# Convolution sums in a PSUM bank, and products between the transposes of a feed-forward block: a two-layer hybrid encoder in float32

## The chip, the cores and the metric

The kernel runs on one core of a Trainium2 chip. The metric is the device time of one execution in microseconds (us); the median of three runs is compared. The engines are TensorE (PE, and PEld for its weight loads), VectorE (DVE), ScalarE (ACT), GpSimd (POOL) and SyncE (SP, which here only starts the weight loads).

## The reference, cut to what matters

Each of two layers works on x, 256 tokens by 1024 channels:

```python
x = x + 0.5 * swiglu_ffn(rms_norm(x, g1), w_gate, w_up, w_down)       # 1024 -> 2816 -> 1024
u = rms_norm(x, g_mix) @ w_in                                         # 1024 -> 2304
z = a * sigmoid(gate)                                                 # 256 channels each, from u
y_conv = silu(layer_norm(depthwise_conv(z, w_dw, width=31) + b_dw))
y_pool = pooled means (windows 2, 4, 8, 16) minus u, a linear map per group, a scale
y_attn = differential attention, 4 heads, softmax(q0 k0) - lam * softmax(q1 k1)
x = x + concat(y_conv, y_pool, y_attn) @ w_out
x = x + 0.5 * swiglu_ffn(rms_norm(x, g2), w_gate2, w_up2, w_down2)
x = rms_norm(x, g_post)
```

The change concerns two places of it: the depthwise convolution, 31 taps for each of 256 channels, and the turn of the hidden activation of the feed-forward block between its up and its down product.

## The kernel before, in words

All weights are streamed from HBM in pieces of 1 MB (`WeightStream`), and each quarter of a piece is split into a high and a low float32r part: ACT casts the high part (`whi`), DVE subtracts to get the low part (`wlo`). A product of float32 accuracy is then three matmuls, high by high, high by low, low by high (`mm3`), issued together.

A feed-forward block (`ffn`, tiles `f0a`, `f0b`, `f1a`, `f1b`: layer 0 or 1, first or second block) goes through the 2816 hidden channels in five chunks of 512 and one of 256. For each chunk it forms gate and up (`g`, `u`), multiplies them into `t`, and turns `t` on TensorE: per 256 channels four transposes of 128x128 fill one PSUM bank `hTr`, from which ACT and DVE take the high and low parts `hh` and `hl`. A chunk of 512 has eight such transposes, a block 44, the kernel 176. The down product `d` reads `hh` and `hl`.

The mixer (`mixer`, tiles `mx`) has the convolution, the pooling, the attention and the output product `w`. For the convolution a group of 128 channels (`conv(g)`, two of them) is projected (`mx_conv`), gated (`mx_ct`) and multiplied on GpSimd into a row padded by 15 on each side, `zpad`. Then 31 instructions on DVE, the taps, each multiply a shifted window of `zpad` by one column of the parameter tile `par` and add it to the running sum `cacc`, 128x256 float32 in SBUF. So each tap but the first (a TENSOR_SCALAR, which also adds the bias) is a SCALAR_TENSOR_TENSOR that reads `zpad` and `cacc` and writes `cacc`. The two groups give 62 taps in a layer. Meanwhile `pool()` computes the windowed means on GpSimd (`mx_s`, `mx_pd`). Attention is made of the projection `mx_qk`, its norm (`mx_qksq` on ACT, `mx_qkf`, `mx_qkn` on DVE), the transposes `mx_qkT`, their split `mx_qkh` and `mx_qkl`, the scores `mx_sc` and so on.

PSUM has eight banks of 128x512 float32: four with the tag `mm` for long products, and four with the tag `at` for everything else: `hTr`, `tr`, `qkT`, `sc`, `aT`, `o`, `cT`, `cB`, `po`.

The order of all instructions is made before anything is issued: `Program` records every operation with its reads and writes, and `schedule()` plans them with costs from `_cost`, four rounds of a backward pass and a greedy forward pass (`_forwards`). The forward pass takes, among the engines, the operation that can start first; among those of one engine that can start at the same time, the one of highest priority. It also knows how many slots each tag has, and lets an operation wait for a slot. The planned order of each engine is then fixed; each engine works in order and waits for semaphores. Since all operations are issued by one line, the profile shows L431 for nearly all of them, and tiles tell them apart.

Of the kernel before, what the change touches and what calls it, by code (L numbers as in the profile page):

```python
# [16 lines left out]
P = 128  # L17
# [178 lines left out]
class RecordedPool:  # L196
    def __init__(self, pool, bufs, psum=False):
        self.pool, self.bufs, self.psum = pool, bufs, psum

    def tile(self, shape, dt, tag, name, bufs=None):  # L200
        return RecordedTile(self.pool, shape, dt, tag, bufs or self.bufs, name, self.psum).view


ENGINES = ("tensor", "vector", "scalar", "gpsimd", "sync")
# [1 line left out]

class Op:
    __slots__ = ("engine", "cost", "calls", "preds", "succs", "tiles", "prio", "start", "end", "table", "left", "est",
                 "lag")


class Program:
# [5 lines left out]
    def __init__(self, tc, nc):  # L218
        self.tc, self.nc = tc, nc
        self.ops = []  # L220
        self.open = None
        self.chains = {}
        self.waits = []
        self.after = set()
        for e in ("tensor", "vector", "scalar", "gpsimd", "sync"):
            setattr(self, e, _Engine(self, e))

# [13 lines left out]
    def add(self, engine, call, cost, reads, writes, table, lag):  # L241
        i = len(self.ops)
        if self.open is None or self.open == "new":
            op = Op()
            op.engine, op.cost, op.calls, op.preds, op.succs, op.tiles = engine, 0.0, [], set(), [], []
            op.table, op.lag = table, lag
            self.ops.append(op)
            if self.open == "new":
                self.open = op
        else:  # L250
            op = self.open
            i -= 1
            assert op.engine == engine
        op.calls.append(call)
        op.cost += cost * (MARGIN if engine in ("vector", "scalar") else 1.0)
        op.preds |= self.after
        for v in self.waits:
            op.preds.update(j for j, _ in v.tile.writes)
        for v in reads:
            b = v.box()  # L260
            for j, w in v.tile.writes:
                if j != i and _overlap(b, w):
                    op.preds.add(j)
            v.tile.reads.append((i, b))
        for v in writes:
            b = v.box()
            for lst in (v.tile.writes, v.tile.reads):
                for j, w in lst:
                    if j != i and _overlap(b, w):
                        op.preds.add(j)  # L270
            v.tile.writes.append((i, b))
        for v in (*reads, *writes):
            if v.tile not in op.tiles:
                op.tiles.append(v.tile)
                v.tile.touches += 1
# [66 lines left out]
    def _forwards(self):  # L342
        ops, lat = self.ops, LAT
        order_in_tag, next_in_tag, slots = {}, {}, {}
        for op in ops:
            for t in op.tiles:
                if t not in order_in_tag:
                    key = (id(t.pool), t.tag)
                    n = next_in_tag.setdefault(key, 0)
                    order_in_tag[t] = (key, n)  # L350
                    next_in_tag[key] = n + 1
                    slots.setdefault(key, [0.0] * t.bufs)
        done_in_tag = dict.fromkeys(next_in_tag, 0)
        left = {t: t.touches for t in order_in_tag}
        allocated = set()
        pending = {e: [] for e in ENGINES}
        free = dict.fromkeys(ENGINES, 0.0)
        tables = None
        for i, op in enumerate(ops):
            op.left, op.est = len(op.preds), 0.0  # L360
            if not op.left:
                pending[op.engine].append(i)
        result = []
        loads = [i for i, op in enumerate(ops) if op.engine == "sync"]

        def slot_time(op):
            t_, want = 0.0, {}
            for t in op.tiles:
                if t in allocated:
                    continue  # L370
                key, n = order_in_tag[t]
                k = want.get(key, 0)
                if key[1] in IN_ORDER and n != done_in_tag[key] + k or len(slots[key]) <= k:
                    return None
                want[key] = k + 1
                t_ = max(t_, sorted(slots[key])[k] + lat)
            return t_

        while len(result) < len(ops):
            best = None  # L380
            for e, lst in pending.items():
                cand = []
                for i in lst:
                    if e == "sync" and i != loads[0]:
                        continue
                    s = slot_time(ops[i])
                    if s is not None:
                        cand.append((max(ops[i].est, s, free[e]), i))
                if not cand:
                    continue  # L390
                t0 = min(c[0] for c in cand)
                if best is None or t0 < best[0]:
                    i = max((c for c in cand if c[0] <= t0 + 1e-6), key=lambda c: (ops[c[1]].prio, -c[1]))[1]
                    best = (t0, e, i)
            assert best is not None, "no instruction can be issued"
            t0, e, i = best
            op = ops[i]
            pending[e].remove(i)
            if e == "sync":
                loads.pop(0)  # L400
            cost = op.cost
            if op.table is not None and op.table != tables:
                tables = op.table
                cost += 1.3
            op.start, op.end = t0, t0 + cost
            free[e] = op.end
            for t in op.tiles:
                if t not in allocated:
                    allocated.add(t)
                    key, _ = order_in_tag[t]  # L410
                    done_in_tag[key] += 1
                    slots[key].remove(min(slots[key]))
                left[t] -= 1
                if not left[t]:
                    slots[order_in_tag[t][0]].append(op.end + op.lag)
            for j in op.succs:
                o = ops[j]
                o.est = max(o.est, op.end + op.lag + (self.SAME[e] if o.engine == e else lat))
                o.left -= 1
                if not o.left:  # L420
                    pending[o.engine].append(j)
            result.append(i)
        return result
# [71 lines left out]
def trunk_kernel(  # L495
# [20 lines left out]
    def bank(name, tag="at"):  # L516
        return ps.tile([P, 512], F32, tag=tag, bufs=4, name=name)

    def slab_tile(name, dt=F32R):
        return slab.tile([P, 512], dt, tag="s", name=name)  # L520
# [41 lines left out]
    def pcol(l, c, n=1):  # L562
        return par[:, l * NPAR + c:l * NPAR + c + n]
# [95 lines left out]
    def ffn(norm, name, on_chunk, by_tokens=False):  # L659
# [11 lines left out]
        for j in range(NCH + 1):  # L671
# [21 lines left out]
                hid.append(s)  # L693
            for i in range(n // 256):
                tr = bank(f"{name}_hTr{j}{i}")
                for b in range(2):
                    for t in range(2):
                        nc.tensor.transpose(tr[:, b * 256 + t * P:b * 256 + (t + 1) * P],
                                            hid[t][:, (i * 2 + b) * P:(i * 2 + b + 1) * P], ident)
                hi, lo = slab_tile(f"{name}_hh{j}{i}"), slab_tile(f"{name}_hl{j}{i}")  # L700
                split(hi, lo, tr)
                hT += [(hi[:, :256], lo[:, :256]), (hi[:, 256:], lo[:, 256:])]
# [29 lines left out]
    def mixer(l, norm, neg_lam, q_gain, sub_gain, on_chunk):  # L732
# [16 lines left out]
            return acc  # L749

        cv = [tmp.tile([P, SEQ], F32, tag="cacc", name=f"{name}_cacc{g}") for g in range(2)]

        def conv(g):

            acc = proj_T(f"conv{g}")
            t = tmp.tile([P, 2, SEQ], F32, tag="gu", name=f"{name}_ct{g}", bufs=4)
            nc.vector.tensor_mul(t, acc.rearrange("p (a b) -> p a b", a=2),
                                 norm.r_bc.unsqueeze(1).to_broadcast([P, 2, SEQ]))
            nc.scalar.activation(t[:, 1], t[:, 1], AF.Sigmoid)
            nc.gpsimd.tensor_tensor(zpad[g][:, PADC:PADC + SEQ], t[:, 0], t[:, 1], op=ALU.mult)  # L760
            for i in range(CW):
                w = pcol(l, C_DW + g * CW + i)
                src = zpad[g][:, i:i + SEQ]
                if i == 0:
                    nc.vector.tensor_scalar(cv[g], src, w, pcol(l, C_DWB + g), op0=ALU.mult, op1=ALU.add)
                else:
                    nc.vector.scalar_tensor_tensor(
                        out=cv[g], in0=src, scalar=w, in1=cv[g], op0=ALU.mult, op1=ALU.add)

        def conv_norm():  # L770

# [391 lines left out]
```

## Time and profile before

| | us |
|---|---|
| median of 3 runs | 963.55 (962.37 to 964.35) |
| the profiled execution: time | 963.92 |
| its span, first to last instruction | 962.1 |
| PE busy, of the span | 938.0 |
| DVE busy | 611.9 |
| ACT busy | 522.9 |
| POOL busy | 62.5 |

The span is what the trace shows; the profiled execution's own time is 1.8 us longer, and 0.4 us above the median of the runs. A step saved in the span is taken to be saved in the time. The mean granted clock of TensorE over the span is 0.992 of full speed.

### The profile page before, as it was taken

How to read it: one execution, taken by the hardware profiler on the slowest of the kernel's cores; microseconds unless marked ns; L12 is line 12 of the kernel's file. 1: busy time of each engine (PE TensorE's matmuls, PEld its weight loads, DVE VectorE, ACT ScalarE, POOL GpSimd, SP SyncE). 2: the span in 40 equal slices, each digit the busy share in tenths (PEclk: the TensorE clock that was granted, in tenths of full speed). 3: DMA queues.
4: the chain of work that ended last, by engine and by line, in shares of the span. 5: the costliest groups of instructions: out<-in, count | busy, mean ns of one | idle time of the engine just before them, and what ended most of it. 6: DMA issues, size and time to landing. Idle time of an engine off the chain costs nothing.

```text
span 962.1 us, 13147 instructions
## 1 busy us (share of the span) xinstructions
PE 938.0 (97%) x4496; PEld 777.8 (81%) x4496; DVE 611.9 (64%) x1152; ACT 522.9 (54%) x1139; POOL 62.5 (6%) x81
## 2 busy tenths in 40 slices
PE   7999999998999999999999999999989999999997
PEld 5888888896778888888888888888967788888885
DVE  6765566659997555576645556665799865555612
ACT  7754445543886644555544455555369764554601
POOL 1000000014210000000000000000412100000000
PEclk9999999999999999999999999999989999999999
DMA  8885658640167555567516556775303655556601
GB/s 293 293 281 190 198 179 276 212 141 19 66 188 265 161 186 195 186 199 267 194 66 197 179 193 192 243 234 169 109 0 133 218 175 197 193 179 200 216 1 44
DMA packets 47907, 171.42 MB, mean 178 GB/s; under 512 B 5344, under 2 KB 5600, under 8 KB 47712
## 3 DMA queue, kind: packets, MB, share of 16 engines
q1 hardware_dynamic: 46656, 167.27, 52.4%
q0 software_dynamic: 608, 2.62, 0.8%
q8 instruction: 35, 0.57, 0.2%
q10 hardware_dynamic: 576, 0.70, 0.2%
q14 instruction: 32, 0.26, 0.1%
HBM read 169.52 MB, written 1.05 MB: 177 GB/s over the span
## 4 chain that ended last, share of the span: by engine, by line
PE 89%; DVE 5%; ACT 3%; issue 1%; DMA 1%; POOL 0%; SPq 0%; POOLq 0%
PE f0a_d L431 6%; PE f0b_d L431 6%; PE f1a_d L431 6%; PE f0a_g L431 6%; PE f0b_g L431 6%; PE f1b_g L431 6%; PE f1a_g L431 6%; PE f1b_u L431 6%; PE f0b_u L431 6%; PE f1a_u L431 6%; PE f0a_u L431 6%; PE f1b_d L431 5%; DVE mx_cacc L431 4%; PE mx_w L431 3%; PE mx_conv L431 2%; PE mx_v L431 2%
## 5 line engine op out<-in xcount | busy, mean ns | idle before, releaser
L431 DVE SCALAR_TENSOR_TENSOR mx_cacc<-zpad,par,mx_cacc 128x256 f32<-128x256 f32 x120 | 56.9, 542 | 0.1
L431 DVE TENSOR_TENSOR f0b_t<-f0b_t,f0b_u 128x512 f32<-128x512 f32 x10 | 6.8, 685 | 25.6 <-PE f0b_u L431 18.7
L431 DVE TENSOR_TENSOR f1b_t<-f1b_t,f1b_u 128x512 f32<-128x512 f32 x10 | 6.8, 685 | 25.0 <-PE f1b_u L431 18.7
L431 ACT ACT_TABLE_LOAD x12 | 15.4, 1283 | 13.2 <-PE f0b_g L431 5.8
L431 DVE SCALAR_TENSOR_TENSOR x<-f1b_d,f1b_rh,x 128x512 f32<-128x512 f32 x4 | 3.0, 750 | 29.3 <-PE f1b_d L431 29.3
L431 POOL DMA_DIRECT2D mx_pwr<-in_pool_w x2 | 1.2, 618 | 310.8 <-PE f1a_d L431 172.3
L431 ACT ACTIVATE fin_sq<-x 128x512 f32<-128x512 f32 x4 | 2.5, 632 | 34.3 <-DVE x L431 34.3
L431 ACT CAST f1a_hh<-f1a_hTr 128x512 fp32r<-128x512 f32 x11 | 6.0, 590 | 26.0 <-PE f1a_hTr L431 26.0
L431 ACT ACTIVATE f1a_t<-f1a_g,n1a_r 128x512 f32<-128x512 f32 x10 | 6.8, 690 | 23.4 <-PE f1a_g L431 23.4
L431 DVE TENSOR_TENSOR f1a_t<-f1a_t,f1a_u 128x512 f32<-128x512 f32 x10 | 6.8, 684 | 18.7 <-PE f1a_u L431 18.7
L431 ACT CAST f1b_hh<-f1b_hTr 128x512 fp32r<-128x512 f32 x11 | 6.0, 590 | 23.2 <-PE f1b_hTr L431 23.2
L431 ACT CAST f0b_hh<-f0b_hTr 128x512 fp32r<-128x512 f32 x11 | 6.0, 590 | 22.9 <-PE f0b_hTr L431 22.9
L431 DVE TENSOR_TENSOR f0a_t<-f0a_t,f0a_u 128x512 f32<-128x512 f32 x10 | 6.8, 684 | 16.9 <-PE f0a_u L431 16.9
L431 POOL TENSOR_TENSOR mx_qkf<-mx_qkf,mhalf 128x8 f32<-128x8 f32 x8 | 14.1, 1777 | 41.5 <-DVE mx_qkf L431 41.5
L431 ACT ACTIVATE mx_e<-mx_e,mx_mx 128x256 f32<-128x256 f32 x32 | 16.1, 506 | 0.6 <-DVE mx_mx L431 0.5
L431 ACT ACTIVATE f1b_t<-f1b_g,n1b_r 128x512 f32<-128x512 f32 x10 | 6.7, 689 | 16.4 <-PE f1b_g L431 16.4
L431 ACT ACTIVATE f0b_t<-f0b_g,n0b_r 128x512 f32<-128x512 f32 x10 | 6.7, 689 | 16.4 <-PE f0b_g L431 16.4
L431 ACT ACTIVATE mx_qksq<-mx_qk 128x64 f32<-128x64 f32 x64 | 13.2, 258 | 4.0 <-PE mx_qk L431 3.9
L431 PE MATMUL mx_qkT<-cst,mx_qkn 128*128 128x128 f32 x32 | 6.8, 303 | 7.5 <-DVE mx_qkn L431 7.5
L431 ACT CAST f0a_hh<-f0a_hTr 128x512 fp32r<-128x512 f32 x11 | 6.0, 590 | 14.9 <-PE f0a_hTr L431 14.8
L431 DVE CUSTOM_DVE_ANT_0 mx_e<-mx_sc,cst 128x256 f32<-128x256 f32 x32 | 12.3, 418 | 2.5 <-PE mx_sc L431 2.5
L431 POOL TENSOR_TENSOR fin_r<-fin_r,mhalf 128x1 f32<-128x1 f32 x2 | 1.9, 934 | 181.3 <-DVE fin_r L431 181.3
(4339 smaller groups left out, 3476.7 us busy)
## 6 DMA issues: line engine op xcount, KB each, us to landing
x<-in_x SPq DMA_DIRECT2D x4, 256.0 KB, 4.9
cst<-in_consts POOLq DMA_DIRECT2D x1, 1024.0 KB, 10.7
post<-in_post_rows POOLq DMA_DIRECT2D x2, 512.0 KB, 3.9
raw0a<-in_weights SPq DMA_DIRECT2D x2, 256.0 KB, 5.3
raw0b<-in_weights SPq DMA_DIRECT2D x2, 256.0 KB, 6.3
raw1a<-in_weights SPq DMA_DIRECT2D x1, 512.0 KB, 7.2
raw1b<-in_weights SPq DMA_DIRECT2D x1, 512.0 KB, 7.9
raw2a<-in_weights SPq DMA_DIRECT2D x1, 512.0 KB, 8.3
```

Source lines behind the costliest of these rows:

```text
L431: getattr(getattr(self.nc, engine), method)(*[a.resolve() if isinstance(a, View) else a for a in args], **{k: a.resolve() if isinstance(a, ...
```

## The change

The running sums of both groups of the convolution now lie in one PSUM bank, `csum`, with the tag `at`, one half for each group; the planner treats the halves as separate. The taps read the sum from PSUM and write it there, except that the last tap of a group writes its result to `cacc` in SBUF as before. `zpad` and `par` stay in SBUF, and the number and the order of taps stay. The bank is taken with the first tap and comes free with the last.

The transposes into `hTr` are marked `apart`. Where the planner has just put a transpose on TensorE, it takes an `apart` transpose next only if nothing else can start at that time. And it now counts 0.04 us more for a transpose that follows a transpose (`_cost` has 0.07 us for each).

```diff
-    def tile(self, shape, dt, tag, name, bufs=None):
-        return RecordedTile(self.pool, shape, dt, tag, bufs or self.bufs, name, self.psum).view
+    def tile(self, shape, dt, tag, name, bufs=None, whole=None):
+        return RecordedTile(self.pool, shape, dt, tag, bufs or self.bufs, name, self.psum if whole is None else whole).view
...
+    @property
+    def transpose(self):
+        return self.calls[0][1] == "transpose"
...
+        transposed = False
...
-                    i = max((c for c in cand if c[0] <= t0 + 1e-6), key=lambda c: (ops[c[1]].prio, -c[1]))[1]
+                    ready = [c for c in cand if c[0] <= t0 + 1e-6]
+                    if e == "tensor" and transposed:
+                        ready = [c for c in ready if not ops[c[1]].apart] or ready
+                    i = max(ready, key=lambda c: (ops[c[1]].prio, -c[1]))[1]
...
             cost = op.cost
+            if e == "tensor":
+                cost += 0.04 if transposed and op.transpose else 0.0
+                transposed = op.transpose
...
                 tr = bank(f"{name}_hTr{j}{i}")
+                nc.apart = True
                 for b in range(2):
                     for t in range(2):
                         nc.tensor.transpose(tr[:, b * 256 + t * P:b * 256 + (t + 1) * P],
                                             hid[t][:, (i * 2 + b) * P:(i * 2 + b + 1) * P], ident)
+                nc.apart = False
...
         cv = [tmp.tile([P, SEQ], F32, tag="cacc", name=f"{name}_cacc{g}") for g in range(2)]
+        cv_sum = ps.tile([P, 512], F32, tag="at", bufs=4, name=f"{name}_csum", whole=False)
...
                 src = zpad[g][:, i:i + SEQ]
+                acc = cv_sum[:, g * SEQ:(g + 1) * SEQ]
                 if i == 0:
-                    nc.vector.tensor_scalar(cv[g], src, w, pcol(l, C_DWB + g), op0=ALU.mult, op1=ALU.add)
+                    nc.vector.tensor_scalar(acc, src, w, pcol(l, C_DWB + g), op0=ALU.mult, op1=ALU.add)
                 else:
                     nc.vector.scalar_tensor_tensor(
-                        out=cv[g], in0=src, scalar=w, in1=cv[g], op0=ALU.mult, op1=ALU.add)
+                        out=acc if i < CW - 1 else cv[g], in0=src, scalar=w, in1=acc, op0=ALU.mult, op1=ALU.add)
```

## Rows read from the trace of the kernel before

**Rows 1.** The page: busy time of each engine; the chain, by engine.

```profile
PE 938.0 (97%) x4496; PEld 777.8 (81%) x4496; DVE 611.9 (64%) x1152; ACT 522.9 (54%) x1139; POOL 62.5 (6%) x81
...
PE 89%; DVE 5%; ACT 3%; issue 1%; DMA 1%; POOL 0%; SPq 0%; POOLq 0%
```

**Rows 2.** By stretch: us; busy PE, PEld, DVE, ACT, POOL; clock; DMA; GB/s.

```profile
9.00:201.50 192.50, 192.50 (x894) 160.37 (x894) 123.55 (x205) 111.85 (x208) 5.21 (x8) 1.00 0.71 235
201.50:290.00 88.50, 83.23 (x479) 69.10 (x478) 80.23 (x202) 58.33 (x189) 22.40 (x27) 0.98 0.31 103
...
673.00:768.00 95.00, 89.94 (x500) 74.23 (x499) 83.63 (x207) 60.51 (x193) 23.07 (x23) 0.95 0.34 114
```

**Rows 3.** Waits of PE, whole span: us in total, times, longest.

```profile
PE mx_qkT L431 <- DVE mx_qkn L431: 7.5, 2, 3.8
```

**Rows 4.** The chain that ended last: start us, us, what.

```profile
67.49 10.88 PE f0a_u L431 x48
...
216.26 17.48 DVE mx_cacc L431 x33
```

**Rows 5.** By stretch, instructions on `mx_cacc` alone: us; PE, PEld, DVE, ACT; clock.

```profile
215.80:225.34 9.54, 0.00 (x0) 0.00 (x0) 9.49 (x13) 0.00 (x0) 1.00 0.18 69
225.34:233.66 8.32, 0.00 (x0) 0.00 (x0) 8.32 (x22) 0.00 (x0) 1.00 0.00 2
```

**Rows 6.** Busy time of all engines in the first of these stretches.

```profile
215.80:225.35 9.55, 9.55 (x44) 7.90 (x43) 9.52 (x15) 0.41 (x1) 8.64 (x12) 1.00 0.18 69
```

**Rows 7.** Timeline of DVE and of POOL from 213 us: start us, us, instruction.

```profile
212.58 0.68 DVE L431 TENSOR_TENSOR wlo40d<-raw40b,whi40d 128x512 fp32r<-128x512 f32 x1
213.18 0.69 DVE L431 TENSOR_TENSOR mx_ct<-mx_conv,n0m_rbc 128x512 f32<-128x512 f32 x1
213.78 0.79 DVE L431 TENSOR_TENSOR wlo41d<-raw41b,whi41d 128x512 fp32r<-128x512 f32 x1
...
213.27 0.74 POOL L431 TENSOR_TENSOR zpad<-mx_ct 128x256 f32<-128x256 f32 x1 [12.19 <-ACT mx_ct L431]
```

**Rows 8.** Groups by form: xcount | busy us, mean ns | idle before us.

```profile
L431 DVE TENSOR_TENSOR f0a_hl<-f0a_hTr,f0a_hh 128x512 fp32r<-128x512 f32 x11 | 7.2, 685 | 2.3 <-ACT f0a_hh L431 2.3
L431 DVE SCALAR_TENSOR_TENSOR mx_e<-mx_e,mx_w 128x256 f32<-128x256 f32 x16 | 7.1, 477 | 0.0
...
L431 DVE SCALAR_TENSOR_TENSOR mx_qkl<-mx_qkT,par,mx_qkh 128x256 fp32r<-128x256 f32 x8 | 3.8, 474 | 0.4 <-ACT mx_qkh L431 0.4
...
L431 DVE TENSOR_TENSOR mx_ya<-mx_osb,mx_ya 128x256 fp32r<-128x256 f32 x8 | 3.3, 418 | 0.2 <-ACT mx_ya L431 0.2
```

**Rows 9.** Last square sum on ACT, then first norm step on DVE (timeline).

```profile
228.57 0.32 ACT L431 ACTIVATION_READ_ACCUMULATOR mx_qksq<-mx_qk 128x1 f32 x1
...
233.66 0.16 DVE L431 TENSOR_TENSOR mx_qkf<-mx_qkms,mx_em 128x8 f32<-128x8 f32 x1
```

**Rows 10.** By stretch, just after the wait, first and second mixer; columns as in 2.

```profile
237.30:240.40 3.10, 3.08 (x9) 2.53 (x10) 3.10 (x8) 0.00 (x0) 0.08 (x1) 0.52 0.00 0
...
708.90:714.50 5.60, 5.60 (x16) 4.44 (x17) 5.21 (x13) 0.84 (x2) 0.82 (x1) 0.50 0.00 0
```

**Rows 11.** Timeline of DVE: first scores, first and second mixer, with idle before.

```profile
247.97 0.42 DVE L431 CUSTOM_DVE_ANT_0 mx_e<-mx_sc,cst 128x256 f32<-128x256 f32 x1 [0.62 <-PE mx_sc L431]
...
720.83 0.42 DVE L431 CUSTOM_DVE_ANT_0 mx_e<-mx_sc,cst 128x256 f32<-128x256 f32 x1 [0.94 <-PE mx_sc L431]
```

**Rows 12.** Timeline of PE: runs of `hTr` transposes, three products after each.

```profile
134.48 1.03 PE L431 MATMUL f0a_hTr<-cst,f0a_t 128*128 128x128 f32 x8
...
136.06 0.27 PE L431 MATMUL f0a_hTr<-cst,f0a_t 128*128 128x128 f32 x1
...
136.87 0.38 PE L431 MATMUL f0a_hTr<-cst,f0a_t 128*128 128x128 f32 x2
...
137.78 0.27 PE L431 MATMUL f0a_hTr<-cst,f0a_t 128*128 128x128 f32 x1
```

More of the change, by code (lines that the diff above doesn't have):

```diff
@@ L208 @@
     __slots__ = ("engine", "cost", "calls", "preds", "succs", "tiles", "prio", "start", "end", "table", "left", "est",
-                 "lag")
+                 "lag", "apart")
+    @property
+    def transpose(self):
+        return self.calls[0][1] == "transpose"
 class Program:
@@ L224, in __init__ @@
         self.after = set()
+        self.apart = False
         for e in ("tensor", "vector", "scalar", "gpsimd", "sync"):
@@ L245, in add @@
             op.engine, op.cost, op.calls, op.preds, op.succs, op.tiles = engine, 0.0, [], set(), [], []
-            op.table, op.lag = table, lag
+            op.table, op.lag, op.apart = table, lag, self.apart
             self.ops.append(op)
```

## The prediction

> **What bounds the kernel now.** I read the page first. PE is busy 97% of the span and holds 89% of the chain that ended last [rows 1], so two questions matter: does the change shorten PE's own work, and does it remove idle time of PE. The table by stretch answers where such idle time is. In the first feed-forward block PE is busy 192.50 of 192.50 us [rows 2], and so it is in the others; there only the length of PE's instructions counts. In the mixers PE is busy 83.23 of 88.50 and 89.94 of 95.00 us, 5.3 and 5.1 us idle, while DVE is busy 80.23 and 83.63 us [rows 2]. The list of waits then names the place: 7.5 us in two waits of up to 3.8, one in each mixer, the transposes `mx_qkT` waiting for DVE's `mx_qkn` [rows 3]. And the chain says what DVE was doing: 17.48 us of it in one piece are taps [rows 4]. So in the mixer the taps stand ahead of what PE waits for.
>
> Then I looked at the taps by themselves. In the 9.54 us from 215.80 there are 13, one every 0.73 us; in the 8.32 us after it 22 are counted, of which the first is the end of the thirteenth, so 21 at 0.396 us [rows 5]. The instructions are the same. What differs is GpSimd: in the slow stretch it is busy 8.64 of 9.55 us with its 12 instructions of the gate and the pooling [rows 6], in the other not at all. The second mixer repeats this, 13 taps in the 9.54 us from 687.35. So 13 taps in each mixer are held up by GpSimd, by 9.54 - 13 x 0.396 = 4.4 us.
>
> Is it every DVE instruction that GpSimd holds up? The two instructions beside the multiply into `zpad`, which reads and writes SBUF, say no: `mx_ct`, which has one input in PSUM, began at 213.18 and took 0.69 us although GpSimd worked from 213.27; the next, a subtract with both inputs in SBUF, took 0.79, where the same subtract at 212.58, before GpSimd began, took 0.68 [rows 7]. One pair is thin evidence, but it points to the second input from SBUF.
>
> **The change, part by part.** *Taps beside GpSimd.* With the sum in PSUM a tap has one tensor in SBUF, `zpad`, and the column of `par`. If the hold-up goes, each mixer's DVE gains the 4.4 us. If it stays, because `zpad` or the column is enough to cause it, the gain is 0: these are the two bounds. I take 4.4, since `mx_ct` also had one SBUF tensor and was not held up.
>
> *Taps in general.* 62 taps in a mixer now read and write PSUM. For reading there are rows: a SCALAR_TENSOR_TENSOR of 256 elements takes 474 ns with one input in PSUM (`mx_qkl`) and 477 with both in SBUF (`mx_e`) [rows 8]. Nothing on DVE writes PSUM in this trace. Lower bound: 3 ns less, that is 0.2 us a mixer. Upper bound: the bank cannot be read and written at once, and the stream of 256 elements passes twice; 256 elements are worth 685 - 418 = 267 ns on a two-input instruction [rows 8], so 62 x 0.267 = 16.6 us a mixer. I take 0, the value for reading, which is the row it is nearest to. The 0.396 us of an undisturbed tap come from a chain in which each tap reads what the one before wrote, so a wait for the write in SBUF is in them already.
>
> [...] The rows on reading do not show a loss (474 against 477 ns), and no row here shows a write. [...]
>
> *What DVE's 4.4 us are worth.* What DVE does next in the first mixer is `mx_qkf` at 233.66. Its input from ACT was done at 228.9 [rows 9]; 4.4 us earlier is 229.3, so DVE does not run into ACT. `mx_qkn` follows 4.4 us earlier too, and PE's wait of 3.8 us goes. With it goes a second loss. In undisturbed work 48 products of 512 columns take 10.88 us, 0.227 each [rows 4]. [...] So PE could be ahead by 3.8 + 1.5 = 5.3 us in the first and 6.6 us in the second mixer, more than DVE's 4.4. DVE is therefore what is late next, and sets the gain: 4.4, plus the waits of DVE for the first scores, 0.62 and 0.94 us [rows 11], which vanish, as PE is 0.9 and 2.2 us further ahead than DVE. That gives 5.0 and 5.3 us. I carry all of it to the end of the mixer, because DVE is the busiest engine after PE there (80.23 of 88.50 us [rows 2]) and each step behind it moves with it; weight loads move too, as they wait for buffers that DVE empties.
>
> *The bank.* Four banks `at` become three while the taps run, from 215.8 to 247.3. In that time only the transposes `mx_qkT` of two heads need banks; the first scores come right after the last tap (248 [rows 11]). I cost it at 0, covered by that order. If the scores had to wait for the bank they would lose what they gain over the taps, at most 5.3 - 4.4 = 0.9 us a mixer.
>
> *Transposes.* The trace has both arrangements. From the start of a run of transposes to the next, with three products between: 134.48 to 136.06 with eight transposes, 136.06 to 136.87 with one, 136.87 to 137.78 with two [rows 12]. Three products are 3 x 0.227 = 0.68. So eight transposes cost 0.90 us, 0.112 each; two 0.23; one alone 0.13. A run costs 0.11 us for each transpose and 0.01 to 0.02 for being a run. The chain shows the 176 transposes in 47 runs (5 of eight, 15 of six, 19 of two, 8 single). If all stood alone there would be 129 more runs: 129 x 0.01 = 1.3 us more, up to 2.6. A single transpose is not cheaper, as the planner's 0.07 against 0.11 would have it. The bound below is that price, 129 x 0.04 = 5.2 us less; I take 1.3 more, from the rows. The later `hh` and `hl` cost nothing: they are read a whole chunk of products later, by the down product.
>
> The sum: 5.0 + 5.3 - 1.3 = 9.0 us off the profiled 963.92, so 954.9; its median is 0.4 lower. I say **954.6 us**.
>
> **The rivals.**
> *A dearer write to PSUM (slower).* Speaks for it: no row shows the write. Against: reading is no dearer. The gain of 10.3 us is gone when 124 taps each cost 0.08 us more (0.396 to 0.48); from there the change is a loss. At the upper bound it is 33 - 10 + 1.3 = 24 us slower, 988; at half of it 971.
> *The hold-up stays (no change).* GpSimd would hold up an instruction with one tensor and a column from SBUF. Speaks for it: `mx_ct` has no column. Then only the transposes count: 963.55 + 1.3 = 964.9.
> *Given back later.* DVE's gain shrinks in a new plan (the bank at its 0.9 us a mixer, another order of norm and taps, with PE's wait only partly gone). At a third to two thirds of 10.3 us: 958 to 962.
> *Single transposes are cheaper* between gate and up products, of which no single one stands in the trace: 963.6 - 10.3 - 5.2 = 948.
>
> **How the numbers follow.** Forecast 0.60; given back 0.13; hold-up stays 0.10; dearer write 0.12; cheaper transposes 0.05. What this kernel's measurement can tell from no change is about 0.2%, 1.9 us: faster means below 961.6. Faster: 0.60 + 0.13 + 0.05 = 0.78; within it: 0.10; slower: 0.12. The forecast's own range is 951 to 958 (bank lost, 1.8; transposes 1.3 dearer; on the other side all of PE's 11.9 us won and no loss on transposes). The range goes on through "given back" to the case without a change and leaves out the dearer write and most of the cheaper transposes: 949.5 to 965.
>
> **What the profile after would show.** Right: the 13 taps beside GpSimd at 0.40 us, as the others; no wait `mx_qkT <- mx_qkn` of microseconds; clock 1.00 after it; products 0.227 apart. `hTr` mostly single, each 0.12 to 0.13 us with its neighbours; feed-forward blocks 0.3 us longer. Wrong: taps at 0.45 us or more away from GpSimd (dearer write); taps still at 0.7 beside it (hold-up stays); a new wait for a bank or on ACT in 230 to 250 us; feed-forward blocks shorter by over 1 us (cheaper transposes).

## The result, and the profile after

The change made the kernel slower. Its median is 968.95 us (968.64 to 969.21, 4 runs) against 963.95 (962.37 to 964.52, 4 runs) for the kernel before, measured on the same chip: a ratio of 1.0054, with a 95% interval of 1.0037 to 1.0072. The prediction was 954.6 us and a range of 949.5 to 965.0, and the time lies above both. The profiled execution has a span of 966.8 us, 4.7 more than before.

First the page of the kernel after: busy time of each engine, then the chain by engine, to be laid beside [rows 1].

```profile
PE 941.3 (97%) x4496; PEld 772.8 (80%) x4496; DVE 614.0 (64%) x1152; ACT 523.1 (54%) x1139; POOL 58.2 (6%) x81
...
PE 86%; DVE 6%; ACT 3%; issue 2%; DMA 1%; POOL 0%; SPq 0%; POOLq 0%; DVEq 0%
```

PE's share of the chain fell from 89% to 86%, DVE's rose from 5% to 6%, and "issue" from 1% to 2%. So the wait for DVE has grown. The list of waits of PE says so directly (total, times, longest):

```profile
PE mx_qkT L443 <- DVE mx_qkn L443: 11.3, 2, 5.6
...
PE mx_aT L443 <- DVE mx_al L443: 0.5, 2, 0.3
PE mx_o L443 <- POOL mx_of L443: 0.3, 2, 0.2
PE mx_o L443 <- ACT mx_osb L443: 0.3, 1, 0.3
```

The wait that was to vanish went from 7.5 us [rows 3] to 11.3, one of about 5.6 in each mixer. What stands ahead of it are still the taps. They are on record in the list of the tile's instructions (durations in ns: least, median, most), and in the timeline of DVE (start us, us, instruction, count):

```profile
L443 DVE SCALAR_TENSOR_TENSOR mx_csum<-zpad,par,mx_csum x116: 478/490/491, 217.3 to 724.9; 128x256 f32<-128x256 f32 x116
```

```profile
216.73 0.54 DVE L443 TENSOR_SCALAR mx_csum<-zpad,par 128x256 f32<-128x256 f32 x1
217.30 0.49 DVE L443 SCALAR_TENSOR_TENSOR mx_csum<-zpad,par,mx_csum 128x256 f32<-128x256 f32 x1
217.90 0.55 DVE L443 TENSOR_SCALAR mx_csum<-zpad,par 128x256 f32<-128x256 f32 x1
218.48 16.77 DVE L443 SCALAR_TENSOR_TENSOR mx_csum<-zpad,par,mx_csum 128x256 f32<-128x256 f32 x32
235.16 0.16 DVE L443 TENSOR_TENSOR mx_qkf<-mx_qkms,mx_em 128x8 f32<-128x8 f32 x1
235.29 1.01 DVE L443 SCALAR_TENSOR_TENSOR mx_csum<-zpad,par,mx_csum 128x256 f32<-128x256 f32 x2
```

From the row of 32 taps one reads the distance of their starts: the last record is 0.49 long, so (16.77 - 0.49) / 31 = 0.525 us. Before, it was 0.73 on the mean beside GpSimd and 0.396 elsewhere [rows 5]. Now it is 0.525 everywhere, beside GpSimd too. That is two results in one. The hold-up is gone: no tap of the 116 is longer than 491 ns, though GpSimd is busy for 5.95 of the first 6.82 us of that row, as the table by stretch shows (columns as in [rows 6]):

```profile
218.48:225.30 6.82, 6.82 (x32) 5.65 (x31) 6.37 (x13) 0.41 (x1) 5.95 (x10) 1.00 0.04 14
```

And each tap now stands by itself. Before, records were 0.475 long and began 0.396 apart, so that they overlapped, as two taps of the second mixer show, which together take 0.87:

```profile
696.90 0.87 DVE L431 SCALAR_TENSOR_TENSOR mx_cacc<-zpad,par,mx_cacc 128x256 f32<-128x256 f32 x2
```

Now a record of 0.490 ends 0.035 us before the next begins. The chain, from 220.06, shows the same as pieces of DVE with "issue" between them (start us, us, what):

```profile
220.06 0.50 DVE mx_csum L443
220.56 0.02 issue
220.59 0.50 DVE mx_csum L443
221.09 0.02 issue
221.11 0.50 DVE mx_csum L443
```

The arithmetic for a mixer: 13 taps gain 0.73 - 0.525, in all 2.7 us; the other 49 lose 0.525 - 0.396 = 0.129 each, in all 6.3. DVE is 3.6 us later instead of 4.4 earlier. Measured, the stretch of the taps, from the first start to the last, grew by 3.2 us in the first mixer (215.82 to 246.88 before, 216.73 to 251.03 after).

PE does not wait for all 62 taps, but for `mx_qkn`. Ahead of its first instruction stand 41 taps before and 43 after, because the planner's order has changed too. So 13 taps gain 2.7, 28 lose 3.6, and two more take 1.05: 2.0 us later, by this sum. From the first tap to `mx_qkn` the traces have 20.77 us before and 22.63 after, 1.9 more, in either mixer, which is what each of PE's two waits has grown by. In before and in after:

```profile
236.59 0.68 DVE L431 TENSOR_TENSOR mx_qkn<-mx_qk,mx_qkf 128x512 f32<-128x512 f32 x1
239.36 0.68 DVE L443 TENSOR_TENSOR mx_qkn<-mx_qk,mx_qkf 128x512 f32<-128x512 f32 x1
```

Last the clock, by stretch, just behind the wait in either mixer (columns as in [rows 2]):

```profile
239.50:245.50 6.00, 5.40 (x15) 4.33 (x16) 5.47 (x12) 0.62 (x2) 0.00 (x0) 0.51 0.01 3
714.50:719.50 5.00, 4.59 (x13) 3.62 (x14) 4.75 (x11) 0.00 (x0) 0.00 (x0) 0.50 0.00 0
```

Behind PE's 5.6 us of idle time the granted clock is again about half, 0.51 over 6.00 us and 0.50 over 5.00, and in the first mixer for longer than before [rows 10].

Where the 4.7 us of span lie, by the starts of the same PE instructions in both traces (the last `mx_conv` product of a layer, the first `f0b_g` or `f1b_g` product behind the mixer):

| stretch | before | after | |
|---|---|---|---|
| to the last `mx_conv`, layer 0 | 212.73 | 213.64 | +0.91 |
| first mixer, to `f0b_g` | 82.43 | 84.67 | +2.24 |
| `f0b`, `f1a`, to the last `mx_conv`, layer 1 | 389.12 | 390.15 | +1.03 |
| second mixer, to `f1b_g` | 85.10 | 85.18 | +0.08 |
| to the end | 192.76 | 193.20 | +0.44 |

In the second mixer the longer wait is offset, because before has there a further stretch at the lower clock, which after does not have. In before:

```profile
759.50:762.50 3.00, 3.00 (x9) 2.33 (x8) 2.75 (x6) 2.24 (x5) 0.00 (x0) 0.50 0.87 289
```

and in after, in the same part of the mixer:

```profile
763.60:766.70 3.10, 3.10 (x16) 2.52 (x15) 3.10 (x7) 1.93 (x4) 0.69 (x1) 1.00 0.97 308
```

The row of before is worth 0.50 x 3.0 = 1.5 us; PE had been busy 3.21 of the 4.50 us ahead of it (755.0 to 759.5). The first row of the table is no effect of the change alone: four of the kernels below, whose instructions up to there are those of before, differ by 0.28 to 0.88.

### The profile page after: what moved, and what is told of

Read it like the earlier page. It is cut to its first block, busy times and chain, and to the rows that moved or that the text cites. A ratio compares the mean times of both kernels' runs of the same rounds, so it can differ in the third digit from the quotient of the medians.

```text
span 966.8 us, 13104 instructions
## 1 busy us (share of the span) xinstructions
PE 941.3 (97%) x4496; PEld 772.8 (80%) x4496; DVE 614.0 (64%) x1152; ACT 523.1 (54%) x1139; POOL 58.2 (6%) x81
## 3 DMA queue, kind: packets, MB, share of 16 engines
HBM read 169.52 MB, written 1.05 MB: 176 GB/s over the span
## 4 chain that ended last, share of the span: by engine, by line
PE 86%; DVE 6%; ACT 3%; issue 2%; DMA 1%; POOL 0%; SPq 0%; POOLq 0%; DVEq 0%
PE f1a_d L443 6%; PE f0a_d L443 6%; PE f0b_d L443 6%; PE f0a_g L443 6%; PE f1b_g L443 6%; PE f0b_g L443 6%; PE f1a_g L443 6%; PE f1b_u L443 6%; PE f0b_u L443 6%; PE f1a_u L443 6%; PE f0a_u L443 6%; PE f1b_d L443 5%; DVE mx_csum L443 5%; PE mx_w L443 3%; PE mx_conv L443 2%
## 5 line engine op out<-in xcount | busy, mean ns | idle before, releaser
L443 DVE SCALAR_TENSOR_TENSOR mx_csum<-zpad,par,mx_csum 128x256 f32<-128x256 f32 x116 | 56.8, 489 | 3.6
L443 PE MATMUL mx_qkT<-cst,mx_qkn 128*128 128x128 f32 x32 | 7.0, 315 | 11.3 <-DVE mx_qkn L443 11.3
L443 PEld LDWEIGHTS mx_qkT<-cst,mx_qkn 128*128 128x128 f32 x32 | 4.6, 159 | 13.6 <-DVE mx_qkn L443 12.1
L443 DVE TENSOR_TENSOR f1a_hl<-f1a_hTr,f1a_hh 128x512 fp32r<-128x512 f32 x11 | 7.6, 689 | 11.3 <-ACT f1a_hh L443 11.2
L443 DVE TENSOR_TENSOR f0b_hl<-f0b_hTr,f0b_hh 128x512 fp32r<-128x512 f32 x11 | 7.6, 689 | 11.0 <-ACT f0b_hh L443 10.9
L443 DVE TENSOR_TENSOR f1b_hl<-f1b_hTr,f1b_hh 128x512 fp32r<-128x512 f32 x11 | 7.6, 690 | 11.0 <-ACT f1b_hh L443 10.9
```

The lines of the kernel that those rows point to most:

```text
L443: getattr(getattr(self.nc, engine), method)(*[a.resolve() if isinstance(a, View) else a for a in args], **{k: a.resolve() if isinstance(a, ...
```

## The experiments

Two theories were on the table. **A, the tap before:** both halves of `csum` lie in one PSUM bank, so each tap waits for the tap just before it, which belongs to the other group, while in before it waited only for the tap two back. **B, a dear PSUM write:** an instruction of DVE that reads and writes a sum in PSUM is longer, wherever it stands.

What the program itself orders speaks for A. This is the order of DVE in the built programs, with the semaphores that each instruction waits for. The first tap of the second sum reads no sum at all; after the change (the third line) it waits for DVE nevertheless, before it waits for GpSimd alone:

```
221 L443 TENSOR_SCALAR mx0_csum_2214<-zpad1_83,par_85 128x256 [waits Pool_49]
222 L443 SCALAR_TENSOR_TENSOR mx0_csum_2214<-zpad1_83,par_85,mx0_csum_2214 128x256 [waits DVE_49]
223 L443 TENSOR_SCALAR mx0_csum_2214<-zpad0_81,par_85 128x256 [waits DVE_49,Pool_49]
```

and before:

```
221 L431 TENSOR_SCALAR mx0_cacc1_2214<-zpad1_81,par_85 128x256 [waits Pool_49]
222 L431 SCALAR_TENSOR_TENSOR mx0_cacc1_2214<-zpad1_81,par_85,mx0_cacc1_2214 128x256 [waits DVE_49]
223 L431 TENSOR_SCALAR mx0_cacc0_2224<-zpad0_89,par_85 128x256 [waits Pool_49]
```

The counts that the later taps wait for, which this list leaves out, say the same: after the change each tap waits for the tap just before it, before for the one two back.

**The sums alone.** Before, with the sums in one bank as in the change and the transposes left alone.

```diff
...
+        cv_sum = ps.tile([P, 512], F32, tag="at", bufs=4, name=f"{name}_csum", whole=False)
...
+                acc = cv_sum[:, g * SEQ:(g + 1) * SEQ]
...
```

> The kernel before with the sums of both groups in one PSUM bank, and nothing of the change to the transposes. Two theories of the tap's 0.525 us after the change (0.396 before, away from GpSimd). Theory A, the wait: in the kernel before, the taps of the two groups alternate, so each waits for the tap two back, which has ended; in one shared bank each waits for the end of the tap just before it. Theory B, the dearer write: a write to PSUM takes 0.13 us more whatever stands around it. Both expect the same here: taps at 0.525 us from start to start, beside GpSimd too, each mixer's taps 2 to 3 us longer in all, and the whole 2 to 4 us slower than before, 966 to 968. If it is the transposes that made the kernel slower, this run is within 1 us of before.

Measured: 966.40 us against 964.03 (ratio 1.0032, 1.0020 to 1.0043). The taps stand as in the change. In its timeline 31 of them take 16.24 us, (16.24 - 0.49) / 30 = 0.525 each:

```profile
217.94 16.24 DVE L431 SCALAR_TENSOR_TENSOR mx_csum<-zpad,par,mx_csum 128x256 f32<-128x256 f32 x31
```

So the part that was to bring 10.3 us costs 3.1 by itself by the ratio (2.4 between the medians). The order of before is kept, with 41 taps ahead of `mx_qkn`, and PE's wait is 9.2 us:

```profile
PE mx_qkT L431 <- DVE mx_qkn L431: 9.2, 2, 4.6
```

**The transposes alone.** Before, with `apart` and the planner's 0.04, the sums in SBUF.

```diff
...
+                cost += 0.04 if transposed and op.transpose else 0.0
...
+                nc.apart = True
...
```

> The change to the transposes alone, the sums in SBUF as before. By the rows of before and after, a single transpose costs about 0.01 us more than one in a run, so 129 more runs cost 1.3 to 2.6 us: 965 to 967, feed-forward blocks 0.3 to 0.6 us longer each. The rival, that the order of the mixer is changed by the planner's 0.04 us and carries a loss of its own, expects a mixer longer by over 1 us with taps at 0.396.

Measured: 965.75 us against 964.03 (ratio 1.0022, 1.0013 to 1.0031), which is 2.1 us by the ratio. The two ratios multiply to 1.0054, that of the whole change: within the intervals the parts add. The feed-forward blocks hold this cost: `f0b` and `f1a` take 390.15 us as after the change, against 389.12, and the last block 193.17 against 192.76, where with the sums alone they take 389.12 and 192.76. That is about 0.5 us a block, 2.0 in all. The mixers are changed as well: two more taps stand ahead of `mx_qkn`, 43 instead of 41, still 0.396 apart, and PE's wait has grown from 7.5 to 9.1:

```profile
PE mx_qkT L443 <- DVE mx_qkn L443: 9.1, 2, 4.6
```

So the rival of that expectation, a changed order of the mixer, is there too, but not in the time of both mixers together, 83.45 and 82.84 us against 82.43 and 85.10: the further stretch at the lower clock in the second is missing here as well.

**Two banks.** Before, with each group's sum in a bank of its own. Taps, their order and their number of PSUM accesses are those of the sums alone.

```diff
+        cv_sum = [bank(f"{name}_csum{g}") for g in range(2)]
...
+                acc = cv_sum[g][:, :SEQ]
...
```

> The kernel before with the sums in PSUM, each group in a bank of its own (two of the four banks with the tag at), nothing of the change to the transposes. Theory A, the wait: each tap waits again for the tap two back, so taps stand at 0.396 us everywhere, beside GpSimd too; DVE gains 4.4 us a mixer, and if two banks are enough for the attention the whole gains 6 to 10 us: 954 to 958. Theory B, the dearer write: taps at 0.525 as in one bank, 966 to 968. If the banks run short, taps at 0.396 with new waits of PE or DVE for a bank in the mixer, and 958 to 966.

Measured: 952.55 us (951.97 to 953.29) against 964.03, a ratio of 0.9887 (0.9872 to 0.9902), somewhat below what was expected. Its list of the tile, its timeline, its table by stretch and its waits of PE:

```profile
L431 DVE SCALAR_TENSOR_TENSOR mx_csum<-zpad,par,mx_csum x116: 480/492/501, 217.3 to 709.9; 128x256 f32<-128x256 f32 x116
```

```profile
218.12 12.63 DVE L431 SCALAR_TENSOR_TENSOR mx_csum<-zpad,par,mx_csum 128x256 f32<-128x256 f32 x32
```

```profile
216.70:225.30 8.60, 8.60 (x40) 7.11 (x39) 8.56 (x23) 0.41 (x1) 7.46 (x12) 1.00 0.22 78
```

```profile
PE mx_qkT L431 <- DVE mx_qkn L431: 0.5, 2, 0.2
```

The records are as long as in the change, 492 against 490 ns, but they begin (12.63 - 0.49) / 31 = 0.392 us apart: they overlap again, beside GpSimd (busy 7.46 of 8.60 us) as elsewhere. B falls here, since these taps read and write PSUM just as often. The length of a record did not show the loss at all; only the distance of the starts did. PE's wait of 7.5 us is 0.5, and the mean clock over the span rose from 0.992 to 0.999.

**One group, then the other.** Before, with the sums in SBUF, but group 0's taps held back until group 1's last one: no tap of the other group stands between two of the same.

```diff
+                nc.after = {last_tap[0]} if last_tap and g == 0 else set()
...
+            if g == 1:
+                last_tap.append(len(nc.ops) - 1)
```

> The kernel before with the sums in SBUF, but the taps of the second group held until the last tap of the first, so that they no longer alternate. Theory A, the wait: taps away from GpSimd stand at 0.52 to 0.53 us from start to start although nothing is in PSUM; the kernel is slower by 5 us or more. Theory B, the dearer write: 0.396 as before, since SBUF is written.

Measured: 961.07 us against 964.03 (ratio 0.9979, 0.9968 to 0.9991), faster where slower was expected. The distance of the taps came out as A has it. A row of its timeline has 18 taps of one group behind one another; GpSimd is idle all the while, from 212.69 to 223.03:

```profile
213.53 9.34 DVE L431 SCALAR_TENSOR_TENSOR mx_cacc<-zpad,par,mx_cacc 128x256 f32<-128x256 f32 x18
```

That is (9.34 - 0.49) / 17 = 0.521 us in SBUF, against 0.525 in a shared bank and 0.396 in alternation. So the price belongs to waiting for the instruction just before, and not to PSUM; what is left for the shared bank itself is 0.004 us. What was wrong is the time expected from it. The hold made the planner start the first group's taps at 209.12 instead of 215.82 and the norm `mx_qkf` at 222.78, behind 25 taps, instead of 233.66, behind 34; PE's wait for `mx_qkn` is a single one of 0.4:

```profile
222.78 0.16 DVE L431 TENSOR_TENSOR mx_qkf<-mx_qkms,mx_em 128x8 f32<-128x8 f32 x1
```

```profile
PE mx_qkT L431 <- DVE mx_qkn L431: 0.4, 1, 0.4
```

**One SBUF tile.** Before, with both sums in the halves of one SBUF tile: is it sharing a tile that orders the taps, or sharing a bank?

```diff
-        cv = [tmp.tile([P, SEQ], F32, tag="cacc", name=f"{name}_cacc{g}") for g in range(2)]
+        cv2 = tmp.tile([P, 2 * SEQ], F32, tag="cacc", bufs=1, name=f"{name}_cacc")
+        cv = [cv2[:, g * SEQ:(g + 1) * SEQ] for g in range(2)]
```

> The kernel before, with both groups' sums in the two halves of one SBUF tile of 128x512; nothing in PSUM, the transposes as before. If it is the shared PSUM bank that orders the taps one behind the other, this changes nothing: taps at 0.396 away from GpSimd and up to 0.88 beside it, 962 to 966 us. If sharing any one tile orders them, the taps stand 0.52 apart away from GpSimd as they do in the shared bank, and the time is 970 or more, since the hold-up beside GpSimd stays as well.

Measured: 963.79 us against 963.78 (ratio 0.9997, 0.9988 to 1.0007). Its taps by stretch, 13 in 9.53 us and then 21 (and the end of one) in 8.32, are those of [rows 5] to 0.01:

```profile
216.60:226.13 9.53, 0.00 (x0) 0.00 (x0) 9.49 (x13) 0.00 (x0) 1.00 0.18 69
226.13:234.45 8.32, 0.00 (x0) 0.00 (x0) 8.32 (x22) 0.00 (x0) 1.00 0.01 2
```

In SBUF the halves of one tile are told apart, with 8.32 / 21 = 0.396 us a tap; in one PSUM bank they are not, with 0.525 in the sums alone. It is the shared bank.

**One group in PSUM.** Before, with group 1's sum in a bank of its own and group 0's in SBUF.

```diff
+        cv_sum = [cv[0], bank(f"{name}_csum1")]
...
```

> The kernel before, with the running sum of the second group alone in a PSUM bank of its own; the first group's sum stays in SBUF, the transposes as before. The taps of the two groups alternate as before, so each waits for the tap two back. If GpSimd holds up a tap only when two of its tensors are in SBUF, then beside GpSimd every other tap is short (about 0.4 us) and every other stays long (up to 0.88), and away from GpSimd all are at 0.39 to 0.40: about half of the gain of 11.4 us that two banks gave, 957 to 961 us. If what helped with two banks was something of the whole mixer and not the tensor of each tap (another order, say), the taps would be alike, all short or all long, and the time 952 to 954 or 964.

Measured: 954.29 us (953.21 to 955.41) against 963.78, a ratio of 0.9902 (0.9885 to 0.9918). That is well over half the gain, so the expected size is a miss. The kind is right in that only taps on `cacc` are held, but not all of them are: of the eight from 217.96 to 224.68, each beside a working GpSimd, the first three took 0.47 us and the others 0.56 to 1.04. In its timeline the taps alternate; from the fourth of the eight on:

```profile
220.32 0.93 DVE L431 SCALAR_TENSOR_TENSOR mx_cacc<-zpad,par,mx_cacc 128x256 f32<-128x256 f32 x1
221.17 0.48 DVE L431 SCALAR_TENSOR_TENSOR mx_csum<-zpad,par,mx_csum 128x256 f32<-128x256 f32 x1
221.56 0.56 DVE L431 SCALAR_TENSOR_TENSOR mx_cacc<-zpad,par,mx_cacc 128x256 f32<-128x256 f32 x1
222.04 0.48 DVE L431 SCALAR_TENSOR_TENSOR mx_csum<-zpad,par,mx_csum 128x256 f32<-128x256 f32 x1
222.44 1.04 DVE L431 SCALAR_TENSOR_TENSOR mx_cacc<-zpad,par,mx_cacc 128x256 f32<-128x256 f32 x1
223.40 0.48 DVE L431 SCALAR_TENSOR_TENSOR mx_csum<-zpad,par,mx_csum 128x256 f32<-128x256 f32 x1
223.79 0.57 DVE L431 SCALAR_TENSOR_TENSOR mx_cacc<-zpad,par,mx_cacc 128x256 f32<-128x256 f32 x1
224.28 0.48 DVE L431 SCALAR_TENSOR_TENSOR mx_csum<-zpad,par,mx_csum 128x256 f32<-128x256 f32 x1
```

From the start of a tap to the next start: 0.85, 0.48, 0.96, 0.49 us behind a tap on `cacc`, 0.39 to 0.40 behind one on `csum`. The hold-up adds up to some 1.3 us in the mixer (these four and one more, over 0.39), not to half of 4.4. Why it is so much less is not shown.

**The change with two banks.** The change as made, transposes too, but with two banks.

```diff
-        cv_sum = ps.tile([P, 512], F32, tag="at", bufs=4, name=f"{name}_csum", whole=False)
+        cv_sum = [bank(f"{name}_csum{g}") for g in range(2)]
...
-                acc = cv_sum[:, g * SEQ:(g + 1) * SEQ]
+                acc = cv_sum[g][:, :SEQ]
```

> The change as made, transposes between products too, but with each group's sum in a PSUM bank of its own. If the two parts only add, the time is that of the two banks alone, 952.6 us, plus the 1.8 us that the transposes cost alone: 954 to 955, near the 954.6 that was predicted for the change; taps 0.39 apart everywhere and no wait of PE for mx_qkn of over 1 us. If the bank that is now missing collides with the transposes' new order, over 957.

Measured: 954.99 us (954.26 to 956.45) against 963.78, a ratio of 0.9911 (0.9896 to 0.9926). The product of two banks and transposes alone, 0.9887 x 1.0022 = 0.9909, says the same. PE's wait:

```profile
PE mx_qkT L443 <- DVE mx_qkn L443: 0.5, 2, 0.2
```

Two lines of source turn a loss of 5.0 us into a gain of 8.8. The lowest median of all is that of two banks with the transposes left as they were, 952.55 us; its interval of the ratio overlaps that of one group in PSUM.

## Why the prediction was wrong, point by point

**What bounds the kernel: right.** The taps stand ahead of `mx_qkn`, and PE's wait for it follows their length both ways: 9.2 us with the taps at 0.525 in the order of before, 11.3 with two more of them ahead of `mx_qkn`, 0.5 with 0.392.

**The hold-up by GpSimd and its end: right.** With the sum in PSUM no tap is held, in the change or with two banks (the longest of the 116 takes 491 and 501 ns). The column of `par` does not bring it back. With that the rival "the hold-up stays" falls. The reading behind it, that it takes a second tensor in SBUF, is not the whole of it. A row of before, which the prediction did not read, is the first tap of the second sum: it reads `zpad` and columns alone, writes SBUF, and took 0.72 us beside GpSimd, against 0.41 where GpSimd was idle (209.12 in the run with one group, then the other):

```profile
216.92 0.72 DVE L431 TENSOR_SCALAR mx_cacc<-zpad,par 128x256 f32<-128x256 f32 x1
```

Which of its accesses is held is not shown.

**Taps in general, taken at 0: this step failed.** The sentence is "The 0.396 us of an undisturbed tap come from a chain in which each tap reads what the one before wrote, so a wait for the write in SBUF is in them already." In before the groups alternate, and a tap reads what the tap two back wrote; the 0.396 us held no such wait. A row ahead of it could have warned me: records of 0.475 us that begin 0.396 apart overlap. Where each tap does read what the one just before wrote, with one group behind the other, they start 0.521 apart and do not. The wait became real in the change because two sums share one bank, of which the planner knew nothing, since it treats the halves as separate. It cost 0.129 us a tap where the term had 0, over the 0.08 from which, by the prediction itself, the change turns into a loss, and under its upper bound of 0.267, an estimate from [rows 8]. The runs with two banks (0.392), with one group behind the other in SBUF (0.521) and with one SBUF tile (0.396) show the cause: the wait for the tap just before, and through the shared bank.

The runs agree on what that wait is: without one on the neighbour taps start 0.392 to 0.396 us apart, with one in the shared bank 0.525, a record of 0.490 and 0.035 more. The program orders the taps by the bank although all of them are on one engine, at 0.129 us a tap.

**The rival "a dearer write to PSUM"** has the sign and the size (its loss begins at 0.08 a tap) but not the mechanism. PSUM by itself is no dearer for these taps: 0.392 us a tap with each sum in a bank of its own, 0.396 in SBUF; a second pass through the bank, which the upper bound supposes, does not show in it.

**What DVE's time is worth: right in the total, in part by luck.** Predicted were 5.0 + 5.3 = 10.3 us for the mixers. With two banks, where the failed step doesn't enter, the kernel gains 10.9 us by the ratio. The profiled mixers are shorter by 4.3 and 7.7 (82.43 to 78.15 and 85.10 to 77.37, by the stretches above), 12.0 in all; of it 1.5 is the stretch of before at 759.5, which the prediction had not read. The clock loss that stands in PE's 5.3 and 6.6 us is 0.48 x 3.1 = 1.5 and 0.50 x 5.6 = 2.8 us by [rows 10]. It goes, as was said (mean clock 0.999 instead of 0.992), and so do the waits of DVE for the first scores. But with two banks, too, 43 taps stand ahead of `mx_qkn`, and DVE reaches it 3.5 us earlier, not 4.4 (17.23 us behind the first tap instead of 20.77). It reaches the first scores 3.2 and 4.6 us earlier, not 5.0 and 5.3 (28.91 us behind the first tap, instead of 32.15 and 33.47). The rest was gained further on in the mixers, for reasons that the prediction did not give.

**The bank at 0: right as to its slot.** Two slots of the four taken during the taps cost nothing that shows: the run with two banks gained more than forecast (10.9 us against 10.3). That a bank is also what the program orders accesses by is what was overlooked there.

**Transposes, 1.3 us and up to 2.6: right for the feed-forward blocks.** Alone they cost 2.1 us, over 129 additional runs 0.016 each (all 176 stand singly in the profile after), between the 0.01 and 0.02 that were read from [rows 12]. In the profile after, single ones follow one another with three products between:

```profile
136.00 0.27 PE L443 MATMUL f0a_hTr<-cst,f0a_t 128*128 128x128 f32 x1
...
136.81 0.27 PE L443 MATMUL f0a_hTr<-cst,f0a_t 128*128 128x128 f32 x1
...
137.61 0.27 PE L443 MATMUL f0a_hTr<-cst,f0a_t 128*128 128x128 f32 x1
...
138.41 0.27 PE L443 MATMUL f0a_hTr<-cst,f0a_t 128*128 128x128 f32 x1
```

That is 0.80 us from one to the next, less 0.68 for the products: 0.12. The rival of cheaper single transposes falls. A block became 0.5 us longer, not 0.3. What the prediction lacks is the mixer: with the new plan two more taps came ahead of `mx_qkn`, and PE's waits grew by 1.6 us even with the sums in SBUF.

**With the failed term set right** the prediction's own sum would have had DVE 3.6 us later at the end of the taps in each mixer, and 0.9 later at `mx_qkn` (13 taps gain 2.7, 28 lose 3.6); the two taps that the new order put ahead of it make that the 1.9 of either wait. PE's two waits grew by 3.8 in all. Against that stand 0.9 us less at the lower clock (5.40 x 0.49 + 4.59 x 0.50 = 4.9 after; 1.5 + 2.8 from [rows 10] and 1.5 of 759.5 before), and shorter waits behind it, 1.1 after (the last three of the list above) against 2.7 in the same list of before (1.0, 1.0 and 0.7, for `mx_o` and `mx_w`). That makes 3.8 - 0.9 - 1.6 = 1.3 of the 2.3 us that the mixers grew by; the other 1.0 is not assigned. Whether two sums in one bank can be had without the wait was not tried.

## What to carry to other kernels

Before calling a chain of instructions on one engine dependent, read whether their records overlap: if they do, as here with records of 0.475 us that start 0.396 apart, neighbours do not wait for each other. What tied the neighbours together here, a shared PSUM bank or another order, made each wait for the end of its neighbour, at 0.129 and 0.125 us a tap. When two sums are updated in turn, give each a bank of its own (0.392 us a tap here, against 0.525 in a shared one), and compare distances of starts, not lengths of records. And look at what stands ahead of the wait on the bounding engine: with one group behind the other the last tap began 14 us later than before (260.81 against 246.88), and the kernel was still faster, because the norm that PE waits for stood behind fewer taps.

## What the runs showed of the hardware that was not expected

- Waiting for the DVE instruction just before costs the same in either memory: from start to start, a tap of 256 float32 elements a partition takes 0.521 us with the sum in SBUF and 0.525 in PSUM, against 0.396 and 0.392 when it waits for the one two back.
- A small instruction fits into that gap without moving the next tap: `mx_qkf` at 235.16 lies between taps 0.525 us apart (234.76 and 235.29).
- GpSimd's hold-up is not a fixed price for a tap: 13 taps on SBUF in a row lost 4.4 us, while with every second tap on PSUM the loss was 1.3, and three of the eight on SBUF were not held at all.
- The first tap, a TENSOR_SCALAR with one SBUF tensor, takes 0.54 us when it writes PSUM (after and two banks); writing SBUF it took 0.40 (the very first of before) to 0.41 (one group, then the other), and 0.72 beside GpSimd.
